# A quarter of the fifth group's modulation rows on VectorE, the second group's weights queued later, and early gate sums set aside sooner, in a two-layer hybrid mixer

## The chip, the cores and the metric

The kernel runs on one core of one Trainium2 chip. The metric is the device time of one execution in microseconds (us); lower is better. Matrix products run on TensorE (PE in the rows; its loading of weights is PEld), element-wise work on VectorE (DVE) and ScalarE (ACT), and SyncE (SP) issues all the transfers that matter here.

## The reference

Two layers work on 256 latent tokens and 256 context tokens of width 2048. Cut to what matters:

```python
shift, scale, gate = jnp.split(jax.nn.silu(c) @ ada_w[l] + ada_b[l], 3, axis=-1)   # the modulation
h  = rmsnorm(x,  norm_g[l]) * (1.0 + scale[:, None]) + shift[:, None]
hc = rmsnorm(xc, norm_g[l]) * (1.0 + scale_c) + shift_c                            # context, from c_ctx
q, k, v, up, uf, g = split_proj(h @ w_in[l])       # q, k, v, pooling, Fourier, SiLU gate
mixed = concat([attention(q, k, v), pool(up), fourier(uf)])
x = x + gate[:, None] * ((mixed * silu(g)) @ w_out[l])
```

The first layer cannot begin its projection before it has shift and scale, which are a product of two vectors (c and c_ctx) with a matrix of 2048 x 4096, 32 MB in all.

## The kernel before

The normalised and modulated input is held transposed, as 16 tiles of 128 channels by 512 tokens, each split into a high and a low part (`h`); each product is three matmuls (high x high, high x low, low x high). The weights are split the same way: ScalarE casts `raw` to `whi`, VectorE subtracts to `wlo` (lines 138 and 139). `raw`, `whi` and `wlo` have three buffers each, so that a weight piece can be loaded when the third one before it has been split, and cast when TensorE has done with the third one before it.

The change lies in the start of layer 0 (`startup`), about the first 165 us. The 16 tiles are worked through in ten groups, `GROUPS = (1, 1, 2, 2, 2, 2, 2, 2, 1, 1)`: the first group has tile 0, the second tile 1, the third tiles 2 and 3, and so on. In the code j counts groups from 0. For each group:

- The modulation rows come in four pieces (`piece`, 1 MB each for a group of two tiles), each the contribution of a quarter of the 2048 input rows. Each piece is multiplied with the silu of c and c_ctx on TensorE (line 981, eight short matmuls). They have four buffers (tag `a0`), so that a piece's load waits for TensorE's work on the fourth one before it.
- The sums are copied by ScalarE (`ev`, line 1018), transposed by TensorE (line 1024: the group's *turn*, as it is called below), reduced by VectorE (`red`, line 1031), completed (`ab`, lines 1039 and 1040), applied (`xn`, line 255), and split into `h`, high part on ScalarE, low part on VectorE.
- `queue` puts the weights of the group on a list of jobs, and `work` takes matmuls (line 932) from it between the pieces, in an order written out by hand: TensorE runs exactly in the order of the program. A job may be taken only when `now` has reached its `ready`.

From the sixth group on (`ND`), the last quarter of the rows isn't a piece for TensorE but is multiplied and summed by VectorE (`dvec`, line 965: eight instructions for a group of two tiles), with a broadcast copy `cq` of silu(c), which is loaded from a DRAM scratch `cd` that `store_cb` and `late["store"]` have written before.

Three kinds of early products are made in this stage. The first weight block for tiles 0 to 7 is summed in `first`, to be finished later (from tile 8 on another block is made for all tiles, `accs`). The gate columns 11 to 13 are summed over the first `KG` tiles only, in `gfirst`, and copied to `gpart`; after the stage, `a_tile` does the other tiles (line 633). From tile `KG` on, and then also for the tiles before it, gate columns 8 to 10 are summed in `early` over all tiles. `gfirst` and `early` have three of the same four PSUM buffers (`sm`), and the fourth is the group's modulation sum.

Of the kernel before, what the change touches and what calls it, by code (L numbers as in the profile page):

```python
# [12 lines left out]
F32 = mybir.dt.float32  # L13
# [7 lines left out]
P = 128  # L21
# [4 lines left out]
T = N + C  # L26
# [4 lines left out]
AHEAD = 400  # L31
ST = 4
KS = 8
ND = (0, 0, 0, 0, 0, 1, 1, 1, 1, 1)
KG = 4
NE = 3
DLOW = -60
LAG_K = 13.0
PFK, QK, Q0 = 2, 1, 1
# [17 lines left out]
def backbone(  # L57
# [24 lines left out]
    V, S, G, PE = nc.vector, nc.scalar, nc.gpsimd, nc.tensor  # L82
# [71 lines left out]
    def store_cb(cvk, tp):  # L154
        PE.transpose(tp, cvk, idt)
        crow = t2("crow", (32, P))
        S.copy(crow, tp)
        dp = ctx.enter_context(tc.tile_pool(name="dp", bufs=1, space=bass.MemoryType.DRAM))
        cd = dp.tile([32, P], F32, name="cd")
        late["store"] = lambda: nc.sync.dma_start(cd, crow)  # L160
        late["cd"] = cd.rearrange("(v k) p -> v (k p)", v=2)
        late["gd"] = dp.tile([KT, P], F32, name="gd")
# [208 lines left out]
    def f4(s, shape, dt=F32R):  # L371
        return late["f4"].tile(list(shape), dt, tag="f4", name=name(s))
# [459 lines left out]
    for g in range(3):  # L832
        load_x(g, 2)
    cq = [f4("cq", (P, 2, 512), F32) for _ in range(2)]
    h0 = H(T, "h")


    def startup():
        st = tc.tile_pool(name="st", bufs=ST)
        with st as st:  # L840
# [45 lines left out]
            accs = []  # L886
            part = ap_.tile([P, 4, T], F32, tag="A1", name="part")
            gpart = ap_.tile([P, 4, T], F32, tag="A0", name="gpart")
            backlog, jobs = [], []

            def rows(ready, ch, bs, k, i, b, s0, s1):
# [28 lines left out]
            def save(dst, src):  # L920
                for t, a in enumerate(src):
                    S.copy(dst[:, t], a)

            def work(n):
                while n > 0 and (backlog or jobs):
                    while jobs and len(backlog) < LOOK:
                        f, *a = jobs.pop(0)
                        f(*a)
                    if not backlog or backlog[0][0] > now[0]:
                        return  # L930
                    _, o, lt, r, s0, s1 = backlog.pop(0)
                    PE.matmul(o, lt, r, start=s0, stop=s1)  # L932
                    if s1 and o is first[-1]:
                        save(part, first)
                    if s1 and o is gfirst[-1]:
                        save(gpart, gfirst)
                    n -= 1

            now = [0]
# [1 line left out]
            def queue(ready, k0, gs):  # L941
                for f, kl in ((main, KS), (gates, KG)):
                    jobs.append((f, ready, (k0 < kl) == (f is main), k0, gs))
                for f, kl in ((main, KS), (gates, KG)):
                    if k0 + gs == kl:
                        for k in range(0, kl, 2):
                            jobs.append((f, ready, f is gates, k, 2))

            k0 = 0
# [35 lines left out]
            def warm(n):  # L985
                for _ in range(n):
                    PE.matmul(first[3][:, :P], ones, ones, start=True, stop=True)

            with tc.manual_schedule(engines={mybir.EngineType.PE}):
                for g in range(3):  # L990
                    stats(g)
                for j, gs in enumerate(GROUPS):
                    a = smt()
                    w_ = 256 * gs
                    npc = 4 - ND[j]
                    raws = []
                    for kk in range(npc):
                        if j == 0 and kk == 1:
                            load_x(3, 1)
                        if j == 1 and kk == 3:  # L1000
                            late["store"]()
                        if kk == npc - 1 and j + 1 < len(GROUPS):
                            dvec(j + 1)
                        raws.append(piece(j, kk))
                        now[0] = 4 * j + kk + 4 - npc
                        if kk + 4 - npc == (PFK if j else 3):
                            queue(4 * j + 4 + (QK if j else Q0), k0, gs)
                        if j == 0 and kk == 2:
                            norm()
                        if j == 0 and kk == 3:  # L1010
                            nc.sync.dma_start(idt, ident)
                        ada_part(a, raws[kk], kk, kk == 0, kk == npc - 1, w_)
                        if j == 1 and kk < 2:
                            warm(3 - 2 * kk)
                        work(RATE * gs // 2)
                    with tc.high_priority(offset=CHAIN if j == 0 else 0):
                        ev = t2("ev")
                        S.copy(ev[:, :w_], a[:, :w_])
                        if j:
                            work(4)  # L1020
                        else:
                            warm(3)
                        for q in range(2 * gs):
                            PE.transpose(a[:, q * P : q * P + P], ev[:, q * P : q * P + P], idt)
                        if j:
                            work(4)
                        else:
                            store_cb(cvk, a[:32, 2 * P : 3 * P])
                            warm(2)
                        red = sp.tile([P, 2, gs, 2], F32, tag="red", name=name("red"))  # L1030
                        V.tensor_reduce(
                            red.rearrange("p w k v -> p (w k) v"), a[:, :w_].rearrange("p (q g r) -> p q r g", g=4, r=32)[:, :, 0:2, :],
                            axis=AX.X, op=ALU.add,
                        )
                        dst = ab[0][:, :, k0 : k0 + gs]
                        bias = adab[:, : 2 * KT].rearrange("p (w k) -> p w k", w=2)[:, :, k0 : k0 + gs]
                        for e in range(ND[j]):
                            V.tensor_add(red, red, abq[:, e, :, k0 : k0 + gs])
                        V.tensor_add(dst, red, bias.unsqueeze(3).to_broadcast([P, 2, gs, 2]))
                        V.tensor_mul(dst[:, 1], dst[:, 1], ng[:, k0 : k0 + gs].unsqueeze(2).to_broadcast([P, gs, 2]))  # L1040
                        for i in range(gs):
                            k = k0 + i
                            for vs in ((0,), (1,)) if k == 0 else ((0, 1),):
                                make_h(h0, k, xk[k // 4][:, k % 4], rstd, 0, vs)
                    k0 += gs
                now[0] = 10 ** 6
                work(LATE)
                pool_tables(0)
                fourier_loads(0)
                work(10 ** 6)  # L1050
                rope_tables(0)
# [131 lines left out]
```

## Time and profile before

| | |
|---|---|
| median of 3 runs | 1072.87 us (1072.81 to 1073.67) |
| the profiled execution | 1073.19 us, with a span of 1071.4 us from first to last instruction |
| TensorE busy | 1047.4 us (98%) |
| VectorE busy | 842.3 us (79%) |
| ScalarE busy | 479.7 us (45%) |
| transfers | 233.63 MB, mean 218 GB/s |

The span is what the rows below show; the 1.8 us that the execution's own time has beyond it lie around the instructions. A time after "idle before" or in square brackets is how long an engine stood before an instruction, with what released it.

### The profile page before, as it was taken

To read this page: it belongs to the slowest core of one execution; us is meant where nothing else is said; L and a number is where in the kernel's file an instruction comes from. 1 tells how busy PE (TensorE), PEld (TensorE's weight loads), DVE (VectorE), ACT (ScalarE), POOL (GpSimd) and SP (SyncE) were. 2 spreads that over 40 slices of the span, in tenths; PEclk is the share of its full clock that TensorE was granted. 3 is DMA by queue.
4 is the path that set the end of the run, shared out by engine and by line. 5 is a ranking of instruction groups with operands and counts; after the bars stand their busy time and mean duration, and the time that the engine had idled before them with its cause. 6 is when DMAs were issued, how large, how long until landed. Compare 5 with 4: busy or idle time off the path is not lost.

```text
span 1071.4 us, 14049 instructions
## 1 busy us (share of the span) xinstructions
PE 1047.4 (98%) x5100; PEld 842.6 (79%) x5100; DVE 842.3 (79%) x1553; ACT 479.7 (45%) x803; POOL 0.2 (0%) x4
## 2 busy tenths in 40 slices
PE   6899999999999999999999999999999999999996
PEld 4466677888787888888888888887888888888885
DVE  6358648998999779998989787489657889776565
ACT  5233225323323766632522223288326767447453
POOL 0000000000000000000000000000000000000000
PEclk9999999999999999999999999999999999999999
DMA  8999777566785244457776667445764565686563
GB/s 336 410 398 343 256 238 242 164 198 214 227 260 169 80 140 158 157 192 273 266 272 213 197 195 265 139 133 169 271 218 161 168 196 185 224 270 212 192 201 117
DMA packets 63797, 233.63 MB, mean 218 GB/s; under 512 B 7104, under 2 KB 8176, under 8 KB 60016
## 3 DMA queue, kind: packets, MB, share of 16 engines
q1 hardware_dynamic: 63152, 231.69, 63.8%
q10 hardware_dynamic: 576, 1.05, 0.3%
q8 instruction: 40, 0.66, 0.3%
q14 instruction: 29, 0.24, 0.1%
HBM read 230.58 MB, written 2.12 MB: 217 GB/s over the span
## 4 chain that ended last, share of the span: by engine, by line
PE 81%; DVE 7%; DMA 4%; ACT 3%; issue 3%; SPq 0%; DVEq 0%; ACTq 0%
PE mm L336 18%; PE mm L335 18%; PE mm L337 18%; PE mm L932 6%; PE mm L311 5%; PE sm L932 3%; DVE ajunk L188 2%; DMA a<-in_ada 2%; PE mm L312 2%; PE sm L336 2%; PE sm L337 2%; PE sm L335 2%; PE sm L981 2%; DVE wlo L139 2%; PE sm L562 1%
## 5 line engine op out<-in xcount | busy, mean ns | idle before, releaser
L138 ACT CAST whi<-raw 128x1024 fp32r<-128x1024 f32 (+1 forms) x216 | 219.9, 1019 | 333.0 <-PE mm L336 112.1
L139 DVE TENSOR_TENSOR wlo<-raw,whi 128x1024 fp32r<-128x1024 f32 (+1 forms) x216 | 255.3, 1182 | 103.7 <-ACT whi L138 102.6
L188 DVE SCALAR_TENSOR_TENSOR ajunk<-araw,cbt 128x1024 bf16<-128x1024 f32 x224 | 273.6, 1221 | 49.8 <-DMA araw<-in_adar 36.9
L335 PE MATMUL mm<-whi,h 128*128 128x512 f32 x416 | 167.6, 403 | 0.0
L336 PE MATMUL mm<-wlo,h 128*128 128x512 f32 x416 | 163.3, 393 | 0.0
L337 PE MATMUL mm<-whi,h 128*128 128x512 f32 x416 | 163.1, 392 | 0.0
L335 PE MATMUL mm<-m,whi 128*128 128x512 f32 (+1 forms) x272 | 102.6, 377 | 0.0
L336 PE MATMUL mm<-m,whi 128*128 128x512 f32 (+1 forms) x272 | 102.4, 377 | 0.0
L337 PE MATMUL mm<-m,wlo 128*128 128x512 f32 (+1 forms) x272 | 102.4, 377 | 0.0
L311 PE MATMUL mm<-h,whi 128*128 128x512 f32 x256 | 92.5, 400 | 0.0
L337 PEld LDWEIGHTS mm<-whi,h 128*128 128x128 f32 x416 | 78.1, 188 | 17.0 <-DVE h L139 0.3
L336 PEld LDWEIGHTS mm<-wlo,h 128*128 128x128 f32 x416 | 78.2, 188 | 16.2 <-issue 1.9
L335 PEld LDWEIGHTS mm<-whi,h 128*128 128x128 f32 x416 | 78.2, 188 | 16.1 <-issue 1.7
L335 PE MATMUL mm<-h,whi 128*128 128x512 f32 x196 | 77.7, 396 | 0.0
L337 PE MATMUL mm<-h,wlo 128*128 128x512 f32 x196 | 76.8, 392 | 0.0
L336 PE MATMUL mm<-h,whi 128*128 128x512 f32 x196 | 76.8, 392 | 0.0
L312 PE MATMUL mm<-h,wlo 128*128 128x256 f32 x256 | 72.4, 283 | 0.0
L932 PE MATMUL mm<-whi,h 128*128 128x512 f32 x192 | 63.8, 401 | 0.2 <-ACT h L138 0.2
L335 PEld LDWEIGHTS mm<-m,whi 128*128 128x128 f32 x272 | 51.2, 188 | 9.5
L337 PEld LDWEIGHTS mm<-m,wlo 128*128 128x128 f32 x272 | 51.2, 188 | 9.4
L336 PEld LDWEIGHTS mm<-m,whi 128*128 128x128 f32 x272 | 51.2, 188 | 9.2
L311 PEld LDWEIGHTS mm<-h,whi 128*128 128x128 f32 x256 | 48.1, 188 | 10.8
(229 smaller groups left out, 1639.1 us busy)
## 6 DMA issues: line engine op xcount, KB each, us to landing
araw<-in_adar SPq DMA_DIRECT2D x128, 512.0 KB, 4.0
raw<-in_wb SPq DMA_DIRECT2D x78, 512.0 KB, 3.6
raw<-in_wg SPq DMA_DIRECT2D x55, 512.0 KB, 4.3
a<-in_ada SPq DMA_DIRECT2D x24, 1024.0 KB, 9.1
raw<-in_wo SPq DMA_DIRECT2D x32, 512.0 KB, 4.3
raw<-in_wot SPq DMA_DIRECT2D x32, 512.0 KB, 3.9
a<-in_ada SPq DMA_DIRECT2D x16, 512.0 KB, 4.6
x<-in_xT SPq DMA_DIRECT2D x4, 1024.0 KB, 8.1
```

What stands on the lines that cost most here:

```text
L138: i = S.copy(hi, src)
L139: V.tensor_sub(lo, src, hi.bitcast(F32))
L188: V.scalar_tensor_tensor(junk, raw, 1.0, cbt[:, v], op0=ALU.mult, op1=ALU.mult, accum_out=acc[:, u, h, v : v + 1])
L311: PE.matmul(a.rearrange("p (s n) -> p s n", s=2), hi[:, j - j0], h.both[k][:, :, :N], start=s0, stop=False)
L312: PE.matmul(a[:, :N], lo[:, j - j0], h.hi[k][:, :N], start=False, stop=s1)
L335: PE.matmul(o, ah, bh, start=start, stop=False)
L336: PE.matmul(o, ah, bl, start=False, stop=False)
L337: PE.matmul(o, al, bh, start=False, stop=stop)
L562: PE.transpose(tp[:, h * P : h * P + P], ps[h][:, i * P : i * P + P], idt)
L932: PE.matmul(o, lt, r, start=s0, stop=s1)
L981: PE.matmul(a[32 * i : 32 * i + 32, :w_], cs[:, 4 * kk + i], raw[:, i], start=first_, stop=last, tile_position=(0, 32 * i))
```

## The change

- `ND` has its first 1 at the fifth group (tiles 6 and 7), not the sixth. That group has three pieces on TensorE; the load of `cq` comes one group earlier, and VectorE gets eight more multiplications.
- `KG` is 2, not 4: gate columns 11 to 13 are summed over tiles 0 and 1 in the stage, and over 14 tiles in `a_tile`. Columns 8 to 10 begin with tiles 0 and 1 as soon as tile 1 is there.
- `gfirst` is copied to `spare`, in the buffers that tiles 14 and 15 of `h` will have, and from there to `gpart` after the third group, when x isn't needed in that place any more.
- The second group's weights are queued behind the first piece of the third group. The transposition for `cd` moves from the first group's turn to the second's, and its store from the second group to the fourth.

```diff
-ND = (0, 0, 0, 0, 0, 1, 1, 1, 1, 1)
-KG = 4
+ND = (0, 0, 0, 0, 1, 1, 1, 1, 1, 1)
+KG = 2
...
+    lent = [hp.tile([P, 2, T], F32, tag=f"h{k}", name=f"lent{k}") for k in (14, 15)]
...
+            spare = [lent[t // 2][:, t % 2] for t in range(NE)]
...
                     if s1 and o is gfirst[-1]:
-                        save(gpart, gfirst)
+                        for t, a_ in enumerate(gfirst):
+                            S.copy(spare[t], a_)
...
-                        if j == 1 and kk == 3:
+                        if j == 3 and kk == 0:
                             late["store"]()
...
-                        if kk + 4 - npc == (PFK if j else 3):
+                        if j == 2 and kk == 0:
+                            queue(8 + QK, 1, 1)
+                        if j != 1 and kk + 4 - npc == (PFK if j else 3):
                             queue(4 * j + 4 + (QK if j else Q0), k0, gs)
...
                         if j:
                             work(4)
                         else:
+                            warm(2)
+                        if j == 1:
                             store_cb(cvk, a[:32, 2 * P : 3 * P])
-                            warm(2)
...
                     k0 += gs
+                    if k0 == 6:
+                        save(gpart, spare)
```

How the order of instructions moves is shown at three places. Line numbers differ between the two (981 became 984, 1024 became 1029, 932 became 934, 965 became 968, 1031 became 1037, 1039 and 1040 became 1045 and 1046).

First, SyncE's transfers in the second and third groups, before (`in_wb` and `in_wgs` are weights, `in_ada` pieces of modulation rows; 128x1024 are those of the second group, 128x2048 those of the third):

```order
L976 DMA a_62_307<-in_ada 128x1024
L145 DMA raw_313<-in_wb 128x512
L145 DMA raw_319<-in_wgs 128x384
L160 DMA cd<-crow_262 32x128
L976 DMA a_69_333<-in_ada 128x1024
L976 DMA a_74_361<-in_ada 128x2048
L976 DMA a_75_367<-in_ada 128x2048
L976 DMA a_76_387<-in_ada 128x2048
L145 DMA raw_393<-in_wb 128x1024
L145 DMA raw_399<-in_wgs 128x768
L976 DMA a_83_412<-in_ada 128x2048
```

and now:

```order
L979 DMA a_61_302<-in_ada 128x1024
L979 DMA a_62_315<-in_ada 128x1024
L979 DMA a_68_350<-in_ada 128x2048
L145 DMA raw_356<-in_wb 128x512
L979 DMA a_81_377<-in_ada 128x2048
L145 DMA raw_362<-in_wgs 128x384
L145 DMA raw_371<-in_wgs 128x768
L979 DMA a_82_397<-in_ada 128x2048
L145 DMA raw_403<-in_wb 128x1024
L145 DMA raw_420<-in_wgs 128x768
L979 DMA a_89_432<-in_ada 128x2048
L160 DMA cd<-crow_333 32x128
```

The second group's last piece and two of the third's have moved ahead of tile 1's weights; a third weight piece (`raw_371`, gate columns 8 to 10 for tiles 0 and 1) has come in between.

Second, TensorE at the fourth group's turn, before (`h_108` to `h_111` are tiles 0 to 3, `sm_454` to `sm_456` the sums of `early`):

```order
L932 MATMUL sm_146<-h_111,whi_401 128x512 x2
L932 MATMUL sm_146<-h_111,wlo_402 128x512
L932 MATMUL sm_454<-h_108,whi_459 128x512 x2
L932 MATMUL sm_454<-h_108,wlo_460 128x512
L932 MATMUL sm_455<-h_108,whi_459 128x512
L1024 MATMUL sm_440<-idt,ev_531 128x128 x4
L932 MATMUL sm_455<-h_108,whi_459 128x512
L932 MATMUL sm_455<-h_108,wlo_460 128x512
L932 MATMUL sm_456<-h_108,whi_459 128x512 x2
L981 MATMUL sm_561<-a_110_562,cs 32x512 x4
L932 MATMUL sm_456<-h_108,wlo_460 128x512
L932 MATMUL sm_454<-h_109,whi_459 128x512 x2
```

and now (`h_113` is tile 3, `h_114` tile 4, which this very turn leads to):

```order
L934 MATMUL sm_370<-h_113,whi_422 128x512 x2
L934 MATMUL sm_370<-h_113,wlo_423 128x512
L1029 MATMUL sm_471<-idt,ev_567 128x128 x4
L984 MATMUL sm_592<-a_115_593,cs 32x512 x4
L934 MATMUL mm_142<-whi_507,h_114 128x512
L934 MATMUL mm_142<-wlo_508,h_114 128x512
L934 MATMUL mm_142<-whi_507,h_114 128x512
```

Before, products of tiles 0 and 1 stood around the turn and behind it; now one piece stands between the turn and the first product of the tile that comes out of it.

Third, VectorE around the same turn, before (`red_545` belongs to it, `h_112` and `h_113` are its tiles):

```order
L248 TENSOR_TENSOR xn_555<-x_1_86,rstd_137 128x512
L139 TENSOR_TENSOR wlo_520<-raw_517,whi_519 128x1024
L1031 TENSOR_REDUCE red_545<-sm_440 128x8
L1039 TENSOR_TENSOR ab_96<-red_545,vt 128x2x4
L1040 TENSOR_TENSOR ab_96<-ab_96,vt 128x4
L255 TENSOR_SCALAR xn_549<-xn_549,ab_96 128x256 x2
L255 TENSOR_SCALAR xn_555<-xn_555,ab_96 128x256 x2
L139 TENSOR_TENSOR h_112<-xn_549,h_112 128x512
```

and now, in two pieces that follow on each other:

```order
L139 TENSOR_TENSOR wlo_525<-raw_522,whi_524 128x768
L968 SCALAR_TENSOR_TENSOR junk_535,abq<-a_104_533,cq_106 128x512
L968 SCALAR_TENSOR_TENSOR junk_538,abq<-a_104_533,cq_106 128x512
L968 SCALAR_TENSOR_TENSOR a_104_533,abq<-a_104_533,cq_106 128x512 x2
L968 SCALAR_TENSOR_TENSOR junk_541,abq<-a_104_533,cq_106 128x512
L968 SCALAR_TENSOR_TENSOR junk_544,abq<-a_104_533,cq_106 128x512
L968 SCALAR_TENSOR_TENSOR a_104_533,abq<-a_104_533,cq_106 128x512 x2
L248 TENSOR_TENSOR xn_577<-x_1_86,rstd_139 128x512
L248 TENSOR_TENSOR xn_583<-x_1_86,rstd_139 128x512
L1037 TENSOR_REDUCE red_573<-sm_471 128x8
```

```order
L1045 TENSOR_TENSOR ab_96<-red_573,vt 128x2x4
L1046 TENSOR_TENSOR ab_96<-ab_96,vt 128x4
L255 TENSOR_SCALAR xn_577<-xn_577,ab_96 128x256 x2
L255 TENSOR_SCALAR xn_583<-xn_583,ab_96 128x256 x2
L139 TENSOR_TENSOR wlo_622<-raw_619,whi_621 128x1024
L139 TENSOR_TENSOR h_114<-xn_577,h_114 128x512
```

The eight multiplications of the fifth group now stand ahead of the fourth group's `red`, behind the split of a gate weight (`wlo_525`), and another weight split (`wlo_622`) stands between `xn` and the low part of tile 4.

## Rows read from the trace of the kernel before

**Rows 1.** Stages: busy us of each engine, instructions, TensorE clock, transfer share, GB/s

```profile
24.00:28.00 4.00, 3.77 (x21) 2.19 (x21) 2.32 (x6) 1.35 (x3) 0.00 (x0) 1.00 0.62 168
52.00:56.00 4.00, 4.00 (x26) 2.70 (x22) 0.48 (x1) 0.84 (x1) 0.00 (x0) 1.00 1.02 420
...
20.00:60.00 40.00, 36.05 (x217) 20.64 (x210) 19.06 (x39) 11.72 (x21) 0.00 (x0) 1.00 0.98 392
...
100.00:160.00 60.00, 60.00 (x311) 41.43 (x311) 35.55 (x89) 15.27 (x23) 0.00 (x0) 1.00 0.73 251
```

**Rows 2.** Chain that ended last: start, us, what

```profile
35.50 11.06 DMA a<-in_ada
...
67.67 3.40 PE sm L932 x14
71.08 0.99 PE sm L981 x8
...
147.49 4.08 PE sm L932 x18
```

**Rows 3.** TensorE in order of time: start, us, instruction, idle before it

```profile
31.70 0.38 PE L1024 MATMUL sm<-idt,ev 128*128 128x128 f32 x2
...
34.38 1.06 PE L981 MATMUL sm<-a,cs 128*32 128x512 f32 x8 [0.90 <-DMA a<-in_ada]
...
43.37 0.66 PE L1024 MATMUL sm<-idt,ev 128*128 128x128 f32 x4 [0.71 <-ACT ev L1018]
...
46.61 1.06 PE L981 MATMUL sm<-a,cs 128*32 128x512 f32 x8 [1.17 <-DMA a<-in_ada]
...
60.62 0.60 PE L1024 MATMUL sm<-idt,ev 128*128 128x128 f32 x4
...
80.63 0.60 PE L1024 MATMUL sm<-idt,ev 128*128 128x128 f32 x4
...
96.09 0.60 PE L1024 MATMUL sm<-idt,ev 128*128 128x128 f32 x4
```

**Rows 4.** SyncE in order of time: when transfers were issued

```profile
23.91 0.33 SPq L145 DMA_DIRECT2D raw<-in_wgs  x1
...
27.78 0.54 SPq L145 DMA_DIRECT2D raw<-in_wb  x1
```

**Rows 5.** VectorE in order of time

```profile
44.13 0.19 DVE L1031 TENSOR_REDUCE red<-sm 128x8 f32<-128x32 f32 x1 [1.53 <-PE sm L1024]
...
46.17 1.34 DVE L139 TENSOR_TENSOR h<-xn,h 128x512 fp32r<-128x512 f32 x2
...
55.52 0.96 DVE L139 TENSOR_TENSOR wlo<-raw,whi 128x768 fp32r<-128x768 f32 x1 [6.10 <-ACT whi L138]
...
60.81 1.22 DVE L139 TENSOR_TENSOR wlo<-raw,whi 128x1024 fp32r<-128x1024 f32 x1 [3.13 <-ACT whi L138]
...
73.15 0.69 DVE L965 SCALAR_TENSOR_TENSOR junk<-a,cq 128x512 f32<-128x512 f32 x1
...
78.05 1.29 DVE L248 TENSOR_TENSOR xn<-x,rstd 128x512 f32<-128x512 f32 x2
```

**Rows 6.** ScalarE in order of time

```profile
21.59 0.25 ACT L157 COPY crow<-sm 32x128 f32<-32x128 f32 x1 [0.27 <-PE sm L155]
...
25.23 0.62 ACT L138 CAST whi<-raw 128x512 fp32r<-128x512 f32 x1 [0.30 <-DMA raw<-in_wb]
...
54.65 0.84 ACT L138 CAST whi<-raw 128x768 fp32r<-128x768 f32 x1 [6.22 <-PE mm L932]
...
58.55 1.27 ACT L922 COPY gpart<-sm 128x512 f32<-128x512 f32 x2 [1.43 <-PE sm L932]
59.73 1.05 ACT L138 CAST whi<-raw 128x1024 fp32r<-128x1024 f32 x1
```

**Rows 7.** TensorE's first matmuls, in order of time

```profile
7.73 1.22 PE L871 MATMUL sm<-sq,ones 128*128 128x256 f32 x2 [7.73 <-DVE sq L868]
...
12.80 0.59 PE L871 MATMUL sm<-sq,ones 128*128 128x256 f32 x2
```

## The prediction

> **What bounds the kernel now.** I read the table of stages first. TensorE is the bound from end to end, but from 20 to 60 us it is busy for only 36.05 of 40.00 us, so 3.95 us are lost there; from 100 to 160 us it loses nothing [rows 1]. The chain of waits then says why: it runs through a transfer of modulation rows that was issued at 35.50 and landed 11.06 us later, and from there on through TensorE alone, in a steady pattern of 14 products (3.40 us) and one piece (0.99 us) [rows 2]. In TensorE's own order of time the waits up to there are 0.90 us for one piece, 1.17 us for another, 0.71 us for the copy ahead of the third group's turn [rows 3]. So the start is bound by transfers until 46.6 us, and later by TensorE's work. The transfers have a hole themselves: 168 GB/s from 24 to 28 us, where later stretches have 420 [rows 1]. SyncE stood there until 23.91 before a weight whose buffer wasn't free, with the next pieces queued behind it [rows 4].
>
> What hides the latency of a turn (copy, transposition, `red`, `ab`, `xn`, split) is a stock of products that need no new tile. I count it from the order written out by hand. Before, at the fourth group's turn, tiles 0 to 3 allow 48 products of the first block, 36 of `gfirst` and 36 of `early`: 120, of which 88 are done, so 32 (7.3 us) are left. At the fifth turn 152 of 162 are done, at the sixth 202. After the change the fourth turn has 48 + 18 + 36 = 102 and all 102 are done; the fifth has 144 of 144. The stock is empty at both turns.
>
> **The change, step by step.** A product takes 4.08 / 18 = 0.227 us [rows 2].
>
> *Work.* One piece less on TensorE: 0.99 us, and 3.40 us for 14 products instead of 14 x 0.227 = 3.17, so 1.22 us are saved. Eighteen products of `gfirst` leave the stage and eighteen come back in `a_tile`: nothing, as long as TensorE is bound there. Their larger splits (0.96 us for 128x768 on VectorE [rows 5], against some two thirds of that before) lie under the 18 products that come with them; uncovered they would cost 3 x 0.3 us.
>
> I now follow TensorE to the sixth turn, because from there it has work without a break as before.
>
> *Second group.* Its last piece and two of the third group's no longer wait behind tile 1's weights, so the hole from 24 to 28 us closes. The turn comes at 31.4 instead of 31.70 [rows 3]. But the transposition for `cd` now hangs on this turn: `red` waits for the copy `crow` (0.25 us [rows 6]), and on VectorE the split of tile 1's weight stands between `red` and `ab`, behind its cast on ScalarE (0.62 us [rows 6]) that stands behind `crow`. Together some 1.4 us come into the chain. From `red` to the first low part a group of two tiles takes 44.13 to 46.17 + 0.67 = 2.71 us [rows 5]; with one tile about 0.7 less. TensorE can start tile 1's products at about 35.6. Before, it started when the piece that came in at 34.38 was done, at 35.4 [rows 3]. The 0.90 us saved there are lost again.
>
> *Third group.* Two patterns of 4.40 us, 0.25 us for the copies that free the buffers of `gfirst` for `early` (some 0.6 us each [rows 6], one of them behind a weight cast; bounds 0 and 1.8), and 11 more products: the turn is at 35.6 + 8.8 + 0.25 + 2.5 = 47.2, against 43.37 [rows 3], with 60 products done instead of 42. Eighteen products are 4.1 us, so this is even. `red` begins 0.76 us after the turn (44.13 against 43.37) and the low part is needed by the third product, so products of tiles 2 and 3 can start 0.76 + 2.71 - 0.46 = 3.0 us after the turn: 50.2. The two pieces in between take as long. The copies from `spare` to `gpart` (3 x 0.64 us on ScalarE) lie in these 3 us ahead of the cast; if that cover fails they cost up to 1.9.
>
> *Fourth group.* Pattern, piece, pattern: 50.2 + 4.4 + 3.4 = 58.0, where the last piece is needed. Its transfer: the weights of tiles 2 and 3 now wait for the splits of tile 1's (33.6 and 36.6) instead of going out from 27.78 [rows 4], and the queue runs dry from 34 to about 38.6 with a short break. Then 8.1 MB stand ahead of that piece's end (four pieces of 1.05 and their weights, `cq`, VectorE's piece, itself). At 0.415 MB per us [rows 1] it lands at about 58.2, with a wait of 0.4 us. Turn at 58.4 + 1.0 + 3.2 = 62.6, against 60.62 [rows 3], with 102 products instead of 88.
>
> *Fourth turn to tiles 4 and 5.* This is the main term. A gate weight's cast takes over the buffer of the first block's weight of tiles 2 and 3 and must wait until TensorE has used it, at 54.6 + 10 x 0.227 = 56.9; the same kind of wait is seen before, 6.22 us long [rows 6]. Then in VectorE's order: cast 0.84, split 0.96, eight multiplications 73.15 to 78.05 = 4.90, two `xn` 1.29 [rows 5, 6], so `red` begins at 64.9 and not at 62.6 + 0.76. After it the low part comes 2.71 us later, plus one more weight split of 1.15 that stands in between; products of tile 4 start at 64.9 + 3.86 - 0.46 = 68.3. TensorE has only one piece (1.0) and the transposition (0.6) for this: it stands for about 4.1 us. If VectorE were in time, 1.5 to 2 us would be left.
>
> *Fifth turn.* 68.3 + 4.4 + 4.4 + 3.2 = 80.3. The weight split between `red` and `ab` needs a cast (1.05 us [rows 6]) whose buffer comes free only with the last product ahead of the turn, so `ab` begins at about turn + 2.3, and products of tiles 6 and 7 start 2.0 later: 84.6. TensorE stands for 2.7 us; without that split, 1.5 to 2.
>
> *Sixth turn.* 84.6 + 8.8 + 18 x 0.227 = 97.5, and a little (0.3) for `red` behind it, against 96.09 [rows 3]: 1.7 us later. And 12 products more are still to come than before (260 + 18 against 266), 2.7 us.
>
> Sum: 1.7 + 2.7 = +4.4 us. The saved piece is in it; the loss is about 9.6 us of standing instead of 3.95. Against the profiled 1073.19 us that is 1077.6. The median of the runs is 0.3 lower, so I predict 1077.3.
>
> **The rivals.** *A, the forecast:* both turns are uncovered and VectorE is late at the fourth. For it: the emptied stock and VectorE's order are in the program, and the durations are rows. Against it: one late transfer shifts the waits about. 1075.2 to 1079.
>
> *B, only the bare latency shows.* If VectorE's piece arrives and is multiplied before the turn, and the splits are done in time, the fourth and fifth turn cost 1.7 us each and not 4.1 and 2.7: 3.4 us less, so 1073.9. For it speaks that transfers may be ahead of my count; against it that the split waits for TensorE, whatever the transfers do. Below +2.15 us (0.2% of the time, about what a measurement can tell from no change) this counts as the same.
>
> *C, faster.* The early gates fill the waits of the third group and tiles 4 to 7 come in time. With nothing lost at either turn the sum is 4.4 - 6.8 = -2.4: 1070.5. It decides at a point: to be faster by 0.2% the two turns together must cost under 0.3 us. The third group's turn before, with an empty stock, cost 0.71 and 1.17 us even with two pieces behind it [rows 3], which speaks against.
>
> *D, the clock.* TensorE's first matmuls after its long idle start took 1.22 us a pair, and from 12.80 on 0.59 [rows 7]: half speed for 4.9 us. Before, no later wait is over 1.17 us, so no row says what one of 2 us or more does. If the new wait at the fourth turn sends the clock back to the lower of its two levels for as long, half of 4.9 us is lost: 1077.3 + 2.4 = 1079.7. The Trainium skill, "TensorE: Matmul & The Clock Gate", section "Why this matters for your kernels", states that idle gaps between bursts of matmuls send TensorE back to the half clock; by it the time would be this case's. The granted clock of 1.00 through the gaps from 20 to 60 us [rows 1] doesn't show it for gaps as short as those.
>
> **How the numbers follow.** A 62%, B 20%, C 8%, D 10%. The likeliest is A, with its 1077.3. B lies within 0.2% but for its upper end (17% and 3%), so faster 8%, same 17%, slower 75%. The range of 8 in 10 takes in B and D and the bounds above (copies +1.5, +1.9), and leaves out C: 1072.0 to 1080.5.
>
> **What would show it.** Right: in the changed profile TensorE stands for 2 us or more in one wait, or two around one piece, between the fourth group's transposition (about 62 to 63 us) and tile 4's products, and for over 2 us after the fifth's (about 80); VectorE's multiplications of the fifth group end just before `red` of the fourth; the sixth turn is near 97.5; no wait for pieces over 0.5 us before 50 us; and the stretch from 100 to 160 us is full. Wrong: `red` right behind the fourth transposition, waits there under 1 us, a sixth turn before 95 us; or a loss behind the stage, where I expect none (`a_tile`'s larger pieces).

## The result, and the profile after

The changed kernel takes 1079.38 us (median of 6 executions, 1077.52 to 1082.4) against 1072.86 us for the one before: ratio 1.0062, 95% interval [1.0046, 1.0077], slower. The prediction was 1077.3 in a range of 1072.0 to 1080.5. The profiled execution took 1080.19 us with a span of 1078.4, 7.0 more than before.

TensorE stands nearly as long as forecast, but it also loses its clock twice. The table of stages, after (columns as in [rows 1]):

```profile
20.00:60.00 40.00, 36.26 (x215) 20.84 (x203) 19.46 (x39) 13.66 (x24) 0.00 (x0) 1.00 0.98 382
60.00:100.00 40.00, 34.51 (x159) 21.61 (x160) 29.02 (x77) 10.26 (x15) 0.00 (x0) 0.91 0.88 340
100.00:160.00 60.00, 59.97 (x316) 40.47 (x315) 36.67 (x91) 17.24 (x25) 0.00 (x0) 1.00 0.76 258
...
68.00:70.00 2.00, 0.95 (x3) 0.51 (x4) 2.00 (x3) 0.92 (x2) 0.00 (x0) 1.00 0.95 328
70.00:72.00 2.00, 2.00 (x6) 1.58 (x6) 0.62 (x2) 0.00 (x0) 0.00 (x0) 0.54 1.00 414
...
88.00:90.00 2.00, 2.00 (x6) 1.61 (x6) 2.00 (x6) 0.00 (x0) 0.00 (x0) 0.50 0.98 397
```

From 100 to 160 us nothing is lost, as before. From 20 to 100 us TensorE stands for 80 - 36.26 - 34.51 = 9.2 us (9.6 were forecast), and in the two stretches at 70 and 88 us it is busy all the time but at 0.5 of its clock, the lower of its two levels: 6 matmuls in 2 us, where 311 in 60 us [rows 1] are some 10.

TensorE in order of time, after, the turns and the waits ([rows 3] before):

```profile
31.52 0.38 PE L1029 MATMUL sm<-idt,ev 128*128 128x128 f32 x2
...
47.37 0.60 PE L1029 MATMUL sm<-idt,ev 128*128 128x128 f32 x4
...
60.53 1.06 PE L984 MATMUL sm<-a,cs 128*32 128x512 f32 x8 [1.84 <-DMA a<-in_ada]
...
64.84 0.60 PE L1029 MATMUL sm<-idt,ev 128*128 128x128 f32 x4
65.91 1.07 PE L984 MATMUL sm<-a,cs 128*32 128x512 f32 x8 [0.47 <-DVE red L1037]
68.44 0.50 PE L934 MATMUL mm<-whi,h 128*128 128x512 f32 x1 [1.47 <-ACT h L138]
...
69.79 0.93 PE L934 MATMUL mm<-whi,h 128*128 128x512 f32 x2 [0.61 <-DVE h L139]
...
83.07 0.60 PE L1029 MATMUL sm<-idt,ev 128*128 128x128 f32 x4
84.02 1.06 PE L984 MATMUL sm<-a,cs 128*32 128x512 f32 x8 [0.35 <-DVE red L1037]
87.14 0.73 PE L934 MATMUL mm<-whi,h 128*128 128x512 f32 x1 [2.05 <-ACT h L138]
...
101.75 0.60 PE L1029 MATMUL sm<-idt,ev 128*128 128x128 f32 x4
```

The second and third turns are where they were forecast. Around the fourth there are 1.84 + 0.47 + 1.47 + 0.61 = 4.4 us of waits, around the fifth 2.4. The chain of waits shows what the clock cost behind each:

```profile
69.79 4.63 PE mm L934 x12
...
87.14 5.05 PE mm L934 x14
```

Twelve products take 4.63 us instead of 12 x 0.227 = 2.7, and fourteen 5.05 instead of 3.40 [rows 2]: 1.9 + 1.65 = 3.5 us.

VectorE and SyncE, after, in order of time, show what stood ahead of the fourth group's `red` and ahead of its last piece:

```profile
59.57 0.68 DVE L968 SCALAR_TENSOR_TENSOR junk<-a,cq 128x512 f32<-128x512 f32 x1
...
64.46 1.29 DVE L248 TENSOR_TENSOR xn<-x,rstd 128x512 f32<-128x512 f32 x2
65.67 0.19 DVE L1037 TENSOR_REDUCE red<-sm 128x8 f32<-128x32 f32 x1
...
67.91 1.23 DVE L139 TENSOR_TENSOR wlo<-raw,whi 128x1024 fp32r<-128x1024 f32 x1 [0.23 <-ACT whi L138]
69.05 1.29 DVE L139 TENSOR_TENSOR h<-xn,h 128x512 fp32r<-128x512 f32 x2
...
84.16 1.23 DVE L139 TENSOR_TENSOR wlo<-raw,whi 128x1024 fp32r<-128x1024 f32 x1
```

```profile
43.74 0.86 SPq L961 DMA_DIRECT2D cq<-cd  x2
44.83 0.33 SPq L964 DMA_DIRECT2D a<-in_ada  x1
49.85 5.82 SPq L979 DMA_DIRECT2D a<-in_ada  x3
```

and the time from issue to landing of VectorE's piece (line 964, issued at 44.83):

```profile
DMA to landing us min/median/max: 13.2/13.2/13.2
```

The copies `cq` and VectorE's piece went out ahead of the fourth group's last piece, which is the first of the three loads from 49.85 on. That load was issued only then, when a buffer came free (VectorE's piece has one of the four), but this cost nothing that shows: VectorE's piece, ahead of it, landed at 58.0, and the last piece 2.5 us later, at 60.5, which is the time of its own 1.05 MB at 420 GB/s. It was late by what stood ahead of it. In gates_order below, without the copies and VectorE's piece ahead, it landed at 56.1.

The eight multiplications ended as forecast just before `red`, but `red` was only 0.83 us behind the turn, because that turn itself was late. What is left of the wait behind the turn is the way from `red` to `h`, with a weight split (67.91) between `xn` and the low part.

### The profile page after: what moved, and what is told of

The parts are those of the page before. It is cut to its first block, busy times and chain, and to the rows that moved or that the text cites. A ratio compares the mean times of both kernels' runs of the same rounds, so it can differ in the third digit from the quotient of the medians.

```text
span 1078.4 us, 14050 instructions
## 1 busy us (share of the span) xinstructions
PE 1049.0 (97%) x5092; PEld 845.0 (78%) x5092; DVE 847.9 (79%) x1569; ACT 481.3 (45%) x805; POOL 0.2 (0%) x4
## 3 DMA queue, kind: packets, MB, share of 16 engines
q10 hardware_dynamic: 576, 1.05, 0.3%
## 4 chain that ended last, share of the span: by engine, by line
PE 93%; DVE 3%; DMA 2%; ACT 1%; issue 1%; SPq 0%; DVEq 0%; ACTq 0%
PE mm L336 21%; PE mm L335 21%; PE mm L337 21%; PE mm L934 7%; PE mm L311 5%; PE sm L934 3%; PE mm L312 3%; PE sm L336 2%; PE sm L335 2%; PE sm L337 2%; PE sm L984 2%; PE sm L562 2%; DMA raw<-in_wb 1%; DVE wlo L139 1%; DMA a<-in_ada 1%; DMA x<-in_xT 1%
## 5 line engine op out<-in xcount | busy, mean ns | idle before, releaser
L138 ACT CAST whi<-raw 128x1024 fp32r<-128x1024 f32 (+3 forms) x215 | 219.7, 1023 | 343.7 <-PE mm L336 131.1
L139 DVE TENSOR_TENSOR wlo<-raw,whi 128x1024 fp32r<-128x1024 f32 (+3 forms) x215 | 255.3, 1188 | 97.7 <-ACT whi L138 95.7
L311 PE MATMUL mm<-h,whi 128*128 128x512 f32 x256 | 92.3, 400 | 0.0
L335 PE MATMUL mm<-h,whi 128*128 128x512 f32 x202 | 80.0, 396 | 0.0
L337 PE MATMUL mm<-h,wlo 128*128 128x512 f32 x202 | 79.2, 392 | 0.0
L336 PE MATMUL mm<-h,whi 128*128 128x512 f32 x202 | 79.2, 392 | 0.0
```

Of the source, the lines that this page charges most:

```text
L138: i = S.copy(hi, src)
L139: V.tensor_sub(lo, src, hi.bitcast(F32))
L311: PE.matmul(a.rearrange("p (s n) -> p s n", s=2), hi[:, j - j0], h.both[k][:, :, :N], start=s0, stop=False)
L335: PE.matmul(o, ah, bh, start=start, stop=False)
L336: PE.matmul(o, ah, bl, start=False, stop=False)
L337: PE.matmul(o, al, bh, start=False, stop=stop)
```

## The experiments

Twelve kernels. *Rows* is `ND`, *gates* is `KG` 2 with `spare`, *order* is the queue order with the moved transposition for `cd`; "late" means that VectorE's rows are issued behind the first piece of their own group. Ratios are to the kernel before; TensorE's busy time and clock are those of each profiled execution.

| run | what is in it | median us | ratio [95%] | busy 20:60 | busy 60:100 | clock 60:100 |
|---|---|---|---|---|---|---|
| changed kernel | rows, gates, order | 1079.38 | 1.0062 [1.0046, 1.0077] | 36.26 | 34.51 | 0.91 |
| only_rows | rows | 1077.72 | 1.0051 [1.0037, 1.0065] | 32.92 | 39.98 | 0.95 |
| only_gates | gates | 1080.32 | 1.0074 [1.0062, 1.0087] | 35.26 | 35.47 | 0.96 |
| only_order | order | 1071.47 | 0.9991 [0.9982, 1.0] | 37.27 | 39.96 | 1.00 |
| keep_busy | all, filler matmuls | 1078.48 | 1.0056 [1.0043, 1.0069] | 35.96 | 37.81 | 0.96 |
| rows_order | rows, order | 1076.81 | 1.0037 [1.0024, 1.0049] | 34.21 | 39.96 | 0.99 |
| gates_order | gates, order | 1077.86 | 1.0049 [1.0036, 1.0062] | 37.57 | 35.84 | 0.91 |
| after_late2 | all, group 5 late | 1078.5 | 1.0056 [1.0043, 1.0068] | 37.57 | 34.78 | 0.91 |
| order_rows_late2 | rows, order, group 5 late | 1074.62 | 1.0016 [1.0006, 1.0025] | 37.32 | 37.97 | 0.96 |
| order_rows_late3 | the same, groups 5 and 6 late | 1071.34 | 0.9988 [0.9979, 0.9997] | 36.97 | 39.43 | 1.00 |
| after_late3 | all, groups 5 and 6 late | 1076.12 | 1.0034 [1.0022, 1.0047] | 37.55 | 35.08 | 1.00 |
| order_rows_late49 | rows, order, groups 5 to 10 late | 1070.82 | 0.9978 [0.9969, 0.9987] | 37.20 | 39.96 | 1.00 |
| after_late49 | all, groups 5 to 10 late | 1073.8 | 1.0013 [1.0004, 1.0023] | 37.57 | 37.23 | 1.00 |

**The parts one by one.** Theory: the emptied stock (the gates) is the loss. Rivals: the rows, or the queue order. First only_rows:

```diff
-ND = (0, 0, 0, 0, 0, 1, 1, 1, 1, 1)
+ND = (0, 0, 0, 0, 1, 1, 1, 1, 1, 1)
```

> The kernel before with one part of the change alone: VectorE takes a quarter of the fifth group's modulation rows, so TensorE has one piece less there. Theory (the loss comes from the emptied stock of products): the stock is as before (88 products done at the fourth turn, 138 at the fifth), so the eight multiplications ahead of red, 4.9 us, are mostly covered, and the saved piece (up to 1.22 us) shows: 1071.6 to 1073, ratio 0.9988 to 1.000, granted clock 1.00 from 60 to 100 us. Rival (VectorE's multiplications ahead of red are the cause by themselves): TensorE stands 2 us or more behind the fourth turn, 1075.5 to 1078, and the clock falls there.

The rival's time came out (1077.72), but not by its mechanism. TensorE in order of time in only_rows:

```profile
58.53 1.94 PE L981 MATMUL sm<-a,cs 128*32 128x512 f32 x8 [3.22 <-DMA a<-in_ada]
...
60.40 0.79 PE L932 MATMUL sm<-h,whi 128*128 128x512 f32 x1
```

The wait isn't behind the fourth turn for VectorE, but ahead of it, for the fourth group's last piece, which before was there at 55.40 without a wait. The stock couldn't help: TensorE works in the order of the program, and there the piece stands ahead of it. And the clock falls during the wait (a piece takes 1.94 us instead of 1.06). My theory was wrong for the rows: they cost by what they put ahead in the transfer queue.

Then only_gates:

```diff
-KG = 4
+KG = 2
...
+            spare = [lent[t // 2][:, t % 2] for t in range(NE)]
```

> The kernel before with the gate accumulators put aside after the second tile alone (KG 2, with the spare buffers); queue order and VectorE's share as before. Theory: the stock is empty at the fourth and fifth turns (102 and 144 products done), VectorE isn't late at the fourth, and two pieces stand behind that turn, so waits of 1 to 2 us remain at each: 1074 to 1078, ratio 1.001 to 1.005; a clock below 0.95 between 60 and 100 us only if one wait passes about 2 us. Rival one (the gates are harmless, the rows or the queue order cost it): 1072.5 to 1073.5. Rival two (the longer a_tile stretch costs it): waits at both turns under 0.5 us and yet 1075 or more, with a_tile longer by over 4.2 us.

Slower than expected by 2.3 us. The trace shows two things that the expectation didn't have. With the old queue order the start loses 1.80, 0.93 and 1.30 us in front of pieces at 30.9, 34.5 and 36.9 us. And at the fifth turn VectorE is late after all, with the sixth group's eight multiplications (76.69 to 81.59) ahead of `red`, which begins at 82.80:

```profile
80.02 0.60 PE L1027 MATMUL sm<-idt,ev 128*128 128x128 f32 x4
...
83.03 1.06 PE L984 MATMUL sm<-a,cs 128*32 128x512 f32 x8 [2.41 <-DVE red L1034]
...
85.86 0.79 PE L934 MATMUL mm<-whi,h 128*128 128x512 f32 x1 [1.77 <-ACT h L138]
```

So it is the piece behind the turn that waits for `red`: it sums into the PSUM buffer that `red` has yet to read. At most four products stand between the transposition and that piece in the program's order, and here, with the stock empty, there are none.

And only_order, with the transposition for `cd` and its store moved as in the change:

```diff
+                        if j == 2 and kk == 0:
+                            queue(8 + QK, 1, 1)
-                        if kk + 4 - npc == (PFK if j else 3):
+                        if j != 1 and kk + 4 - npc == (PFK if j else 3):
```

> The kernel before with the queue order alone: the second tile's weights behind pieces of the third group, and the transposition for cd at the second group's turn. Theory: stock as before (42 products done at the third turn, 88 at the fourth), the hole from 24 to 28 us closes, what is saved there is lost at the second turn: 1071.9 to 1073.9, ratio 0.999 to 1.001, with the first modulation wait under 0.6 us and products of tile 1 starting within 0.5 us of before. Rival (the later transfers of the weights are the main cost): the fourth group's last piece is waited for over 1 us and the time is 1075 or more.

As expected, and 0.4 us below the range: the wait for the first pieces is gone, tile 1's products start at 35.03, and the second wait at 46 us (1.17 before [rows 3]) is gone too. The order alone is worth about 1 us, at the edge of what is measured.

**The clock.** Theory: the waits send it down. In keep_busy `zt` is a tile of zeros, so that the fillers add nothing to the sum:

```diff
+                        if j in (4, 5) and kk == 0:
+                            for _ in range(2):
+                                for i in range(4):
+                                    PE.matmul(
+                                        a[32 * i : 32 * i + 32, :w_], zt, raws[0][:, i], start=False, stop=False, tile_position=(0, 32 * i)
+                                    )
```

> The changed kernel with eight more matmuls on a zeroed weight right behind the first piece of the fifth and of the sixth group (they add zero to that group's sum), so that TensorE works through most of the two waits. Theory (the two waits send the clock down, and that costs 1.9 and 1.65 us): the granted clock stays at 1.00 from 66 to 94 us, the 12 to 14 products behind each wait take 0.23 us each again, and the time falls to 1075.5 to 1077.5, 0.996 to 0.9985 of the changed kernel's, with less spread between runs. Rival (the clock falls for another reason): clock 0.91 from 60 to 100 us as in the changed kernel, and 1079 to 1082.

Half of it came, and the time lies between the two ranges. From 66 to 94 us the clock stayed at 1.00, and the wait behind the fifth turn's fillers was 0.33 us. But in this execution the wait for the late piece, ahead of both places, was 3.06 us instead of 1.84, and the clock fell there instead. The table of stages of keep_busy:

```profile
58.00:61.00 3.00, 0.00 (x0) 0.00 (x0) 3.00 (x8) 0.00 (x0) 0.00 (x0) 1.00 1.02 429
62.00:65.00 3.00, 3.00 (x11) 2.38 (x8) 3.00 (x8) 0.59 (x1) 0.00 (x0) 0.52 0.99 412
66.00:94.00 28.00, 26.86 (x150) 15.24 (x149) 20.73 (x56) 7.40 (x11) 0.00 (x0) 1.00 0.87 327
```

So the fall goes with the waits: with the two waits filled, it is gone from both places, and every other fall in the runs here stands behind a wait of some 2 us or more, or a pair of shorter ones. That fillers win time back is not shown: 1078.48 against 1079.38 lies within the spread.

**Pairs.** The changed kernel without the gates, rows_order:

```diff
-KG = 2
+KG = 4
```

> The changed kernel with KG back at 4 and without the spare buffers: VectorE's rows and the queue order are left, the stock of products is that of before (88 products done at the fourth turn). Theory after the first runs (the rows cost through their transfer: the two copies of cd, 0.5 MB, and VectorE's piece, 1.0 MB, with the piece that is left over, stand ahead of the fourth group's last piece in the queue, 1.5 to 2 MB or 3.7 to 5 us late): TensorE waits 2 to 4 us for that piece at 54 to 58 us, the clock falls behind it, 1075.5 to 1078. Rival, the theory of the prediction (only the emptied stock costs): no wait over 1 us there, 1070 to 1072.

The new theory held. TensorE at the fourth group's last piece in rows_order, with no wait from there to 100 us:

```profile
57.68 1.94 PE L981 MATMUL sm<-a,cs 128*32 128x512 f32 x8 [3.11 <-DMA a<-in_ada]
```

The changed kernel without the rows, gates_order:

```diff
-ND = (0, 0, 0, 0, 1, 1, 1, 1, 1, 1)
+ND = (0, 0, 0, 0, 0, 1, 1, 1, 1, 1)
```

> The changed kernel with ND as before, so that only KG 2 and the queue order are left. Theory (empty stock at the fourth and fifth turns costs by itself): the fourth group's last piece comes in time and red follows the fourth turn at once; TensorE stands 1 to 1.5 us behind that turn, and over 3.5 us around the fifth, where the sixth group's eight multiplications stand ahead of red; clock 0.90 to 0.95 from 80 to 100 us; 1075 to 1078. Rival (VectorE's rows cost all): 1072 to 1074.

As expected but for one number. The fourth turn costs 0.35 us, because two pieces stand behind it and cover the latency (1 to 1.5 were expected); the fifth 2.42 + 1.39, with `red` behind the sixth group's multiplications, and the clock is at 0.50 from 82 to 88 us:

```profile
78.31 0.60 PE L1029 MATMUL sm<-idt,ev 128*128 128x128 f32 x4
81.32 1.44 PE L984 MATMUL sm<-a,cs 128*32 128x512 f32 x8 [2.42 <-DVE red L1037]
...
84.16 0.80 PE L934 MATMUL mm<-whi,h 128*128 128x512 f32 x1 [1.39 <-ACT h L138]
```

So VectorE was late at the fifth turn without any of the new rows.

The two losses don't add up. Over only_order (1071.47), the rows cost 5.3 us (rows_order), the gates 6.4 (gates_order), but both together 7.9 (the changed kernel). In the changed kernel the turns come so late that VectorE is done by then: `red` begins 0.83 us behind the fourth and 0.70 behind the fifth.

**VectorE's rows issued later.** The transfer and its multiplications move together; shown is the edit of after_late2 and order_rows_late2, in late3 it holds for j 4 and 5, in late49 for j 4 to 9:

```diff
+                        if j == 4 and kk == 1:
+                            dvec(4)
-                        if kk == npc - 1 and j + 1 < len(GROUPS):
+                        if kk == npc - 1 and j + 1 < len(GROUPS) and j != 3:
                             dvec(j + 1)
```

> The changed kernel with the fifth group's transfer of VectorE's rows (and the two copies of cd) issued behind that group's first piece instead of ahead of the fourth group's last one; its eight multiplications then stand behind the fourth turn's h. Theory (late transfer at the fourth group and the multiplications ahead of its red are about 3.5 us of the loss with their share of the clock, the empty stock at both turns the rest): the wait of 1.84 us for the fourth group's last piece goes below 0.5, red follows the fourth turn by under 1 us, 1.5 to 2.2 us of standing remain there, the fifth turn stays as it is; 1075 to 1077.5. Rival (all of the loss is the empty stock): 1079 to 1080.

At the fourth turn there is no wait for the piece and `red` is 0.70 us behind the turn, as expected; 0.35 + 0.76 us of standing are left, less than expected. But the time hardly moved and lies 1 us above the range, because the loss went to the fifth turn. That came 5 us earlier, at 78.10, and found VectorE still at the sixth group's multiplications, until 79.7 (2.42 + 1.68 us of standing, and the clock at 0.50). "The fifth turn stays as it is" was wrong.

> The kernel before with the queue order of the change and VectorE's rows for the fifth group, whose transfer is issued behind that group's first piece; the gate accumulators stay at the fourth tile. Theory: the saved piece (1.22 us) comes on top of the 1.1 us that the queue order alone gave, with no wait over 0.5 us from 46 to 100 us and the clock at 1.00: 1069.3 to 1071.2, ratio 0.997 to 0.9985. Rival (sixteen multiplications one behind the other make the fifth turn's red late, by over 5 us, so that the stock there, 24 products, doesn't cover it): TensorE stands over 1 us around 80 us, 1072 to 1075.

The rival's time. TensorE at the fifth turn of order_rows_late2, where 24 products of the stock were still to be had:

```profile
75.34 0.60 PE L1028 MATMUL sm<-idt,ev 128*128 128x128 f32 x4
...
78.85 1.77 PE L981 MATMUL sm<-a,cs 128*32 128x512 f32 x8 [2.00 <-DVE red L1036]
```

A stock of products does not cover a late `red`: the next group's first piece stands in TensorE's order ahead of them.

> As the run before with the queue order and the late transfer of VectorE's rows, and now the sixth group's rows are also issued behind that group's own first piece, so that only eight multiplications stand ahead of the fifth turn's red and not sixteen. Theory (red late by 2 us, at whose end the next group's first piece hangs whatever the stock holds, and the clock behind it, were the whole loss of that run): no wait over 0.5 us from 46 to 100 us, clock 1.00, 1069.3 to 1071.2, ratio 0.997 to 0.999. Rival (the sixteen now stand ahead of the sixth turn's red, or the rows come late): a wait of over 1 us at 80 or at 95 us, 1072 to 1075.

The theory's time to within 0.15 us, with 0.54 us left at the sixth turn, where the rival's sixteen had moved to.

> The changed kernel with VectorE's rows of the fifth and of the sixth group issued behind the first piece of their own group: KG 2 and the empty stock stay, VectorE is in time at both turns. Theory (the empty stock by itself costs only the bare latency, about 1 to 1.7 us of standing at each turn, and the rest of the loss is VectorE's multiplications ahead of red, the late piece and the clock behind these): red within 1 us of the fourth and of the fifth turn, clock 1.00 or near it, 1073 to 1075. Rival (the empty stock costs most of it): over 3 us of standing around the fifth turn, 1076.5 or more.

Between the two: the fourth and fifth turns cost 1.1 and 1.7 us, as the theory had it, but the sixth 2.15, for the sixteen multiplications there:

```profile
98.20 1.06 PE L984 MATMUL sm<-a,cs 128*32 128x512 f32 x8 [2.15 <-DVE red L1039]
```

So the last step spreads the late issue over all groups, without and with the gates:

> Queue order and VectorE's rows, KG 4, with VectorE's rows of every group from the fifth to the tenth issued behind the first piece of their own group: never more than one group's multiplications ahead of a red. Theory: the 0.54 us before the sixth turn's next piece goes, waits between 46 and 125 us are under 0.4 us, clock 1.00: 1070.2 to 1071.4, ratio 0.9975 to 0.999. Rival (rows issued so late come late at the later turns, where a group lasts only 8 us): a wait of over 1 us behind 100 us, 1072 to 1074.

> The changed kernel with the same late issue of VectorE's rows for the fifth to the tenth group; KG 2 and the empty stock stay. Theory (the bare latency of the empty stock, 1.1 us at the fourth and 1.7 us at the fifth turn, plus the longer later stretch, is what is left): the wait of 2.15 us at the sixth turn goes below 1.2, no fall of the clock, 1073.5 to 1075.2. Rival (VectorE's lateness wasn't what the last 2 us hung on): 1076 or more, as in the run before.

Both as the theory had them. TensorE in order_rows_late49, with no wait at any of the three turns:

```profile
59.61 0.60 PE L1028 MATMUL sm<-idt,ev 128*128 128x128 f32 x4
...
61.18 1.07 PE L981 MATMUL sm<-a,cs 128*32 128x512 f32 x8
...
75.23 0.60 PE L1028 MATMUL sm<-idt,ev 128*128 128x128 f32 x4
...
76.68 1.06 PE L981 MATMUL sm<-a,cs 128*32 128x512 f32 x8
...
90.70 0.60 PE L1028 MATMUL sm<-idt,ev 128*128 128x128 f32 x4
```

and in after_late49, with the bare latency of the empty stock:

```profile
63.93 1.07 PE L984 MATMUL sm<-a,cs 128*32 128x512 f32 x8 [0.35 <-DVE red L1039]
65.75 0.50 PE L934 MATMUL mm<-whi,h 128*128 128x512 f32 x1 [0.75 <-ACT h L138]
...
79.09 1.07 PE L984 MATMUL sm<-a,cs 128*32 128x512 f32 x8 [0.35 <-DVE red L1039]
81.11 0.50 PE L934 MATMUL mm<-whi,h 128*128 128x512 f32 x1 [0.96 <-ACT h L138]
...
82.20 0.73 PE L934 MATMUL mm<-whi,h 128*128 128x512 f32 x2 [0.35 <-DVE h L139]
```

order_rows_late49, 1070.82 us, is faster than the kernel before (0.9978 [0.9969, 0.9987]) and by 8.6 us than the changed one.

## Why the prediction was right, and where it was off

The sign held, and of the mechanism the main part: both turns stood uncovered. VectorE's rows were in the way too, but at the fourth turn by their transfer and not, as forecast, by their multiplications. The size was off by 2.1 us. The time lies nearer to rival D's 1079.7, which had one chance in ten, than to the forecast's 1077.3. The steps, in order:

- **Second and third turn** (31.4, 47.2): 31.52 and 47.37. Right, with the hole closed and its gain lost again at the second turn.
- **Fourth group's last piece** ("lands at about 58.2, with a wait of 0.4 us"): it landed at 60.5 and cost 1.84. The sum had the bytes, but not the weak stretch of transfers below: from 51 to 54 us 0.5 MB less than at 420 GB/s were moved, which is 1.2 of the 2.3 us. Where the rest comes from is open. With the clock that falls behind it, this wait is the only loss that only_rows and rows_order show from 47 to 100 us.
- **Fourth turn to tiles 4 and 5** ("the main term", 4.1 us for `red` behind eight multiplications): by the forecast's own terms 1.5 us of the 4.1 are the late `red` (64.9 against 62.6 + 0.76), and 2.6 are the way from `red` to the products, with the weight split in it (its "1.5 to 2 us" for VectorE in time leaves the split out). TensorE stood 0.47 + 1.47 + 0.61 = 2.55 us there, which is what the way alone was to cost. `red`, at 65.67, was hardly late: with the turn 2.2 us later, the multiplications lay under the delay of the piece. The late piece and the latency together took 4.4 us, where 0.4 + 4.1 were forecast. The forecast didn't foresee that one delay would cover the other, so that the sum is right is in good part luck.
- **Fifth turn** (2.7 us): 2.4, with the weight split behind `red` (84.16) as forecast.
- **The clock**, rival D with 2.4 us: it fell, in two places, for 3.5 us in the profiled execution. This term is what the forecast missed. The one execution at a mean clock of 0.998, as high as before, took 1077.52 us. With the gates and VectorE in time it stays at 1.00 in the profiled execution (after_late49), but two of that kernel's eleven executions, at mean clocks of 0.996 and 0.995, took 1.8 and 2.0 us more than the median.
- **Sixth turn** (97.5 and 0.3): 101.75. The clock is 3.55 us of the difference.
- **Behind the stage** ("12 products more, 2.7 us"): from the sixth turn to the end the loss grows from 5.66 (101.75 against 96.09) to 7.0 us, so by 1.3. The products came as counted, but a wait of 1.00 us for VectorE at 336 us (line 525) is no longer there with the longer `a_tile`, as in the other runs with gates of 2.

The sum for the profiled execution was +4.4 and came out +7.0: 3.55 for the clock, 0.4 for the rest of the way to the sixth turn, -1.35 behind it. For the medians it was +4.4 against 6.5.

Rival B, the bare latency alone, was priced at 1073.9: after_late49, the nearest run to that case, took 1073.8. That it agrees to 0.1 us is in part chance, as the two turns cost 1.1 and 1.7 us there and not 1.7 each. Gates of 2 against 4, all else equal, cost 1073.8 - 1070.82 = 3.0 us. To the first product behind the stage (line 335, at 167.80 against 168.23 us) the 18 products less, 4.1 us, have brought 0.43; from there to the end, with the 18 in `a_tile`, it takes 3.4 us more.

What the prediction's picture lacked is the second path at a turn. It saw products that need the new tile, which a stock covers; the piece of the next group needs only `red`, but it stands at most four products behind the turn, and no stock covers it.

## What to carry to other kernels

Work that is moved to a less busy engine brings its transfer and its place in that engine's order along: here 1.5 MB ahead of a needed piece cost 6.4 us (only_rows with the saved 1.22 us added), about half of it the wait and half the clock behind it. Issued two pieces later, together with the rows of the groups that follow, the same rows cost nothing (order_rows_late3 and order_rows_late49). Ask of each turn which instruction waits first in program order, and not only how much independent work is left. Where a kernel's new waits come near 2 us, as here, price the clock too.

## What the runs showed of the hardware

**The clock fell behind waits of 2 us and more, but not behind every one.** The granted clock went to 0.50 behind single waits of 2.00 us (order_rows_late2), 2.05 (changed kernel), 2.42 (gates_order and after_late2), 3.06 (keep_busy), 3.11 and 3.22 (rows_order and only_rows; in only_rows already during the wait), and behind 1.47 + 0.61 us with two matmuls in between. It stayed at 1.00 behind 1.84 us in the changed kernel and 2.15 us in after_late3, and behind 2.41 us in only_gates until the wait of 1.77 us that followed. In the changed kernel the two falls cost 1.9 and 1.65 us. The six executions of the changed kernel show it as spread: 1077.52 us at a mean clock of 0.998 to 1082.4 at 0.993. The Trainium skill, "TensorE: Matmul & The Clock Gate", section "Why this matters for your kernels", says that idle gaps between bursts of matmuls bring the half clock back. These traces agree, but the wait of 2.00 us in order_rows_late2 is shorter than the gaps that the section warns of; here the measurement decides.

**A stretch of weak transfers with busy engines.** Before the two copies `cq` (256 KB each, every partition reading the same 2 KB) land, the transfer engines are busy but move little. The table of stages of only_rows:

```profile
50.00:51.00 1.00, 1.00 (x9) 0.57 (x11) 0.00 (x0) 0.00 (x0) 0.00 (x0) 1.00 1.13 313
51.00:52.00 1.00, 1.00 (x9) 0.17 (x2) 0.00 (x0) 0.00 (x0) 0.00 (x0) 1.00 0.97 133
52.00:53.00 1.00, 1.00 (x5) 0.82 (x6) 0.00 (x0) 0.00 (x0) 0.00 (x0) 1.00 0.95 332
```

At a share of 0.97 they move 133 GB/s, where 420 is usual [rows 1]. In the changed kernel it is 254 GB/s from 51 to 54 us, in the kernel before, with the copies some 13 us later, only a dip to 305. By their bytes the copies should take 1.2 us; here 0.48 MB less than at 420 GB/s pass in these three. That the shared source is the cause was not tried.
